# Hybrid SSD/GLA layer: the last block's final state updates left out, the last head's copies and scalings marked as high priority, and its two stores issued by GpSimd

## The chip, the cores and the metric

The kernel runs on 1 core of one Trainium2 chip. The metric is the device time of one execution in microseconds. Before the change it is 2318.2 us, the median of three runs (2316.95, 2318.2 and 2320.6).

A core has the engines TensorE (PE, matmuls; its weight loads are shown as PEld), VectorE (DVE), ScalarE (ACT), GpSimd (POOL) and SyncE (SP), which here only issues DMAs. ACT, too, issues DMAs, as instructions in its own stream (shown as ACTq). Each engine executes its instructions in order.

## The reference, cut to what matters

One layer (DEPTH = 1) over 16 meta tokens and 2048 real tokens, model width 1024. `u` is the normalised input, `proj = u @ w_in` feeds two branches; both carry a state from one chunk of tokens to the next, starting with the meta tokens:

```python
# SSD branch: 4 groups of 4 heads x 64 columns, chunk of 128 tokens
def step(s, inp):
    st, dec = inp
    return dec[..., None, None] * s + st, s          # state for the NEXT chunk
final, prev = lax.scan(step, state0, (states, chunk_decay))
y_off = einsum('bzthn,bzhpn,bhzt->bzthp', cc, prev, exp(da_cum))
return (y_diag + y_off), final
...
y_r, _ = ssd_chunked(...)                            # the last state is not used

# GLA branch: 4 heads, 128 key columns and 256 value columns each
def step(s, inp):
    qi, ki, vi, gi = inp
    o = (qi * exp(gi)) @ s + att(qi, ki, gi) @ vi
    s_new = exp(g_last)[..., None] * s + k_dec.T @ vi
    return s_new, o
...
o_r, _ = gla_chunked(...)                            # the last state is not used

y_gla = rmsnorm(o, gla_norm_w) * silu(g_gla)
merged = sum over branches of sigmoid(gate_b(u)) * (y_b @ w_branch[b])
out = rmsnorm(h + merged @ w_out, final_norm_w)      # float32 throughout
```

## The kernel before, in words

**Numbers.** A float32 product is made of three passes on PE: each operand is split into a high and a low part of type fp32r, and the helper `accum` (L189, L190, L191) sums hi*hi, lo*hi and hi*lo in PSUM. Small products (L594, L595, L597, L847) are plain float32 matmuls; the trace counts each as 2 instructions.

**Phase 1** (tile pools called `first`) goes over 4 blocks of 512 tokens (`nblk`), each of 4 chunks of 128 tokens (`NCH`). A block has 8 units: 4 SSD groups (`ssd_proj`, then `ssd_scan`) and 4 GLA heads (`gla_proj`, then `gla_scan`). They are generators: while one unit projects on PE, `step` lets the scans of earlier units go on one `yield` at a time. In `ssd_scan`, `after(c)` makes the output of chunk c (L594, L595) and the state behind it: a matmul (L597), a decay on POOL (L599) and an addition on DVE (L600). In `gla_scan` the last loop (L842 to L854) makes, for each chunk, in one PSUM bank `po`: the state product `kdt` x v in its right half (L845), the output in its left half (L846, L847), the state update on DVE (L848), a copy of the output to `ot` (ACT, L850) and the sum of its squares (ACT, L852). Then come the reciprocal root (`rstd_of`: DVE L232, POOL L233), four scalings of `ot` (ACT L857), eight transposes (PE L863, four for each half j), a product with the gate for each half (DVE L864, tile `gg`), and two stores of 256 KB into the scratch tensors `y_<block>_<number>` (L867, issued by ACT). For the last head of the last block these are y_3_6 and y_3_7; they are read again only for the last sums of the second branch, much later.

**Phase 2** (pools called `second`) has 7 stages (gate, branch 0 and branch 1 for each half of the tokens, then the output projection), each a row of block products by a scheme with 7 in place of 8 multiplications. A stage reads 28 right-hand tiles: `load_b` (L955, SP) into the raw ring `br` of 5 buffers, `prep_b` splits it by a copy on ACT (L960) and a subtraction on DVE (L961). The left-hand tiles: `load_a` (L967, SP) into the ring `ar` of 8 buffers, sums on POOL (L975 to L978), and `prep_a` splits them on ACT (L984) and DVE (L985). `product` is PE (`accum` again, bank `psa` or `psb`), with a snapshot on ACT (L1001) behind some. A gate stage adds on DVE (L1012), takes tanh on ACT (L1019) and stores with a DMA that ACT issues (L938).

**What sets the order.** PE and SP execute in the order of the code (`manual_schedule`). The instructions of ACT, DVE and POOL are put in order by a scheduler, which plays the program through with its own costs; `tc.high_priority()` puts what stands in it ahead of what else is ready there. Where phase 1 ends, ACT and DVE already hold phase 2's first `prep_a`, ahead of or between the last head's steps. A tile of phase 2 lies in memory that phase 1 had, and waits for whoever used it last.

**Counters of the DMAs.** The DMAs that SP and ACT issue take turns, in the scheduler's order over both engines, on eight completion counters, DMAHW0 to DMAHW7. A DMA whose counter is still out waits until the transfer that had it before, eight DMAs earlier, has landed. DMAs that POOL issues have counters of their own (DMASW).

## Time and profile before

| what | value |
|---|---|
| median of 3 runs | 2318.2 us (2316.95 to 2320.6) |
| the profiled execution's own time | 2309.24 us |
| its span (first to last instruction) | 2307.5 us |
| TensorE clock granted, mean | 0.993 |
| PE busy | 2229.4 us, 97% of the span |
| DVE, ACT, POOL busy | 1623.4, 1119.5, 682.3 us (70%, 49%, 30%) |
| DMA | 515.89 MB, mean 224 GB/s |

An answer of the trace is read as follows. A row of a timeline has the start in us from the span's start, the duration, the engine, the line, the operation, output<-input, size, xcount (instructions that were grouped), and in brackets how long the engine was idle ahead of it and who ended that. A row of a table by windows has the window, its length, then busy time and instructions of PE, PEld, DVE, ACT and POOL, the granted TensorE clock, the busy share of the DMA engines and GB/s. Phase 1 ends and phase 2 begins at about 1501 us; this place is called the seam below.

### The profile page before, as it was taken

The page shows a single profiled execution, that of the slowest core. Times are in us where ns is not written, and L with a number is a line of the kernel's source. Part 1 is how long each engine was busy: PE and PEld are TensorE (multiplying, and loading weights), DVE is VectorE, ACT ScalarE, POOL GpSimd, SP SyncE. Part 2 cuts the span into 40 slices and gives each one's busy share as a digit, 9 for nine tenths or more (in the row PEclk, how much of TensorE's full clock was granted, in tenths as well). Part 3 has the DMA queues.
Part 4 walks back from the last instruction along what each step waited for, and adds up shares of the span by engine and source line. Part 5 has one row for each costly group of instructions (what it writes and reads, how often), then busy time and mean ns, then how long its engine had stood idle before and what let it go on. Part 6 is the DMA issues. An engine that isn't in the chain of part 4 may idle for free.

```text
span 2307.5 us, 36497 instructions
## 1 busy us (share of the span) xinstructions
PE 2229.4 (97%) x12651; PEld 1947.3 (84%) x12651; DVE 1623.4 (70%) x3144; ACT 1119.5 (49%) x2508; POOL 682.3 (30%) x677
## 2 busy tenths in 40 slices
PE   6899999999999999999999999989999999999998
PEld 6899988888889889888988898868788788787886
DVE  5787866687775677676578666664679854788876
ACT  5565654454444454444455334464554455454443
POOL 3344433122221122211122100136424264423341
PEclk9999999999999999999999999999999999999999
DMA  7766865667786676886667655466768866778653
GB/s 255 230 220 214 305 228 204 201 203 233 261 279 197 204 229 204 266 279 208 205 216 228 206 166 162 143 212 214 236 230 270 290 222 215 251 260 271 226 192 110
DMA packets 300937, 515.89 MB, mean 224 GB/s; under 512 B 27616, under 2 KB 143584, under 8 KB 300752
## 3 DMA queue, kind: packets, MB, share of 16 engines
q1 hardware_dynamic: 221840, 422.15, 56.1%
q10 hardware_dynamic: 78912, 91.41, 11.4%
q8 instruction: 99, 1.62, 0.3%
q14 instruction: 86, 0.70, 0.1%
HBM read 366.26 MB, written 147.19 MB: 223 GB/s over the span
## 4 chain that ended last, share of the span: by engine, by line
PE 68%; DVE 11%; DMA 9%; issue 5%; ACT 3%; POOL 2%; SPq 1%; ACTq 0%; DVEq 0%; POOLq 0%
PE pj L189 11%; PE pj L191 11%; PE pj L190 11%; PE psa L189 5%; PE psa L190 5%; PE psa L191 5%; PE psb L189 2%; PE psb L190 2%; PE psb L191 2%; PE pc L594 2%; DMA acc<-in_xmt 2%; PE pc L757 1%; DVE acc L508 1%; PE psc L189 1%; PE psc L190 1%
## 5 line engine op out<-in xcount | busy, mean ns | idle before, releaser
L189 PE MATMUL pj<-u,whl 128*128 128x512 f32 (+1 forms) x1184 | 445.5, 376 | 9.4 <-ACT acc L504 4.9
L191 PE MATMUL pj<-u,whl 128*128 128x512 f32 (+1 forms) x1184 | 430.1, 363 | 0.8 <-POOL whl L177 0.8
L190 PE MATMUL pj<-u,whl 128*128 128x512 f32 (+1 forms) x1184 | 429.3, 363 | 0.0
L189 PE MATMUL pj<-whl,u 128*128 128x256 f32 (+1 forms) x992 | 288.7, 291 | 3.2 <-ACT u L252 2.2
L191 PE MATMUL pj<-whl,u 128*128 128x256 f32 (+1 forms) x992 | 282.4, 285 | 0.2 <-DVE u L257 0.2
L190 PE MATMUL pj<-whl,u 128*128 128x256 f32 (+1 forms) x992 | 282.1, 284 | 0.4 <-POOL whl L177 0.4
L189 PE MATMUL psa<-b,a 128*128 128x512 f32 x640 | 252.4, 394 | 19.3 <-ACT sn L1001 15.8
L189 PEld LDWEIGHTS pj<-u,whl 128*128 128x128 f32 x1184 | 224.1, 189 | 47.9 <-ACT acc L504 5.7
L191 PEld LDWEIGHTS pj<-u,whl 128*128 128x128 f32 x1184 | 223.6, 189 | 36.6 <-POOL whl L177 1.1
L190 PEld LDWEIGHTS pj<-u,whl 128*128 128x128 f32 x1184 | 224.3, 189 | 33.2
L190 PE MATMUL psa<-b,a 128*128 128x512 f32 x640 | 251.3, 393 | 0.0
L191 PE MATMUL psa<-b,a 128*128 128x512 f32 x640 | 251.0, 392 | 0.0
L985 DVE TENSOR_TENSOR a<-ar,a 128x512 fp32r<-128x512 f32 x160 | 158.8, 1000 | 74.2 <-ACT a L984 73.9
L80 POOL TENSOR_TENSOR wr<-wr 128x256 f32<-128x256 f32 x80 | 68.4, 855 | 440.1 <-DMA wr<-u 179.8
L189 PEld LDWEIGHTS pj<-whl,u 128*128 128x128 f32 x992 | 189.6, 191 | 4.3 <-ACT u L252 2.4
L177 POOL TENSOR_TENSOR whl<-wr,whl 128x512 fp32r<-128x512 f32 (+1 forms) x100 | 136.5, 1372 | 190.7 <-ACT whl L176 151.4
L190 PEld LDWEIGHTS pj<-whl,u 128*128 128x128 f32 x992 | 189.8, 191 | 1.0 <-POOL whl L177 0.6
L191 PEld LDWEIGHTS pj<-whl,u 128*128 128x128 f32 x992 | 189.6, 191 | 0.8 <-DVE u L257 0.8
L961 DVE TENSOR_TENSOR b<-br,b 128x512 fp32r<-128x512 f32 x196 | 148.9, 781 | 40.2 <-ACT b L960 39.6
L975 POOL TENSOR_TENSOR as<-ar,ar 128x512 f32<-128x512 f32 x40 | 58.0, 1450 | 399.5 <-DMA ar<-in_w_br 134.2
L508 DVE SCALAR_TENSOR_TENSOR acc<-cin,hcw,acc 128x512 f32<-128x512 f32 (+1 forms) x192 | 159.4, 830 | 13.9 <-ACT acc L504 11.8
L960 ACT ACTIVATE b<-br 128x512 fp32r<-128x512 f32 x196 | 118.9, 626 | 94.3 <-DMA br<-br_t 33.0
(280 smaller groups left out, 5026.6 us busy)
## 6 DMA issues: line engine op xcount, KB each, us to landing
whl<-k_s SPq DMA_DIRECT2D x96, 512.0 KB, 4.4
whl<-k_g SPq DMA_DIRECT2D x96, 512.0 KB, 4.1
whl<-k_v SPq DMA_DIRECT2D x48, 512.0 KB, 4.1
whl<-k_z SPq DMA_DIRECT2D x36, 512.0 KB, 4.2
wr<-in_w_feat SPq DMA_DIRECT2D x64, 256.0 KB, 4.3
k_s<-whl SPq DMA_DIRECT2D x32, 512.0 KB, 3.7
cb<-cumd ACTq DMA_DIRECT2D x64, 256.0 KB, 5.8
y<-gg ACTq DMA_DIRECT2D x64, 256.0 KB, 4.7
```

Of the source, the lines that this page charges most:

```text
L80: nc.gpsimd.tensor_tensor(o, x, y, op=ALU.subtract)
L177: nc.gpsimd.tensor_tensor(hl[:, 1], raw, hl[:, 0].bitcast(F32), op=ALU.subtract)
L189: nc.tensor.matmul(ps, sh, mh, start=first, stop=False, **kw)
L190: nc.tensor.matmul(ps, sh, ml, start=False, stop=False, **kw)
L191: nc.tensor.matmul(ps, sl, mh, start=False, stop=last, **kw)
L508: nc.vector.scalar_tensor_tensor(acc, cin[:, k:k + tt], hcw[:, ti, k:k + 1], acc, op0=ALU.mult, op1=ALU.add)
L594: nc.tensor.matmul(py[:, h * 64:(h + 1) * 64], dm[:, h], xdt[:, h], start=True, stop=True)
L757: nc.tensor.matmul(ps[:, r * P:(r + 1) * P], kq[:, 2 * r * P:(2 * r + 1) * P], kq[:, (2 * r + 1) * P:(2 * r + 2) * P], start=True, stop=True)
L960: nc.scalar.activation(t[:, 0], raw, AF.Copy)
L961: nc.vector.tensor_tensor(t[:, 1], raw, t[:, 0].bitcast(F32), op=ALU.subtract)
L975: nc.gpsimd.tensor_tensor(s1, a21, a22, op=ALU.add)
L985: nc.vector.tensor_tensor(t[:, 1], src, t[:, 0].bitcast(F32), op=ALU.subtract)
```

## The change

1. In `ssd_scan`, `after(c)` leaves out L597, L599 and L600 for the last chunk of the last block (in each of 4 groups).
2. In `gla_scan`, the loop leaves out the `kdt` product (L845, 3 PE instructions) and the state update (L848) for the last chunk of the last block (in each of 4 heads). Both states are read by nobody after that.
3. For the last head of the last block, the state updates, copies, sums of squares, reciprocal root and scalings (L848 to L857) stand in `tc.high_priority()`.
4. That head's two stores are issued by GpSimd in place of ScalarE.

```diff
@@ -593,11 +593,12 @@
             for h in range(4):
                 nc.tensor.matmul(py[:, h * 64:(h + 1) * 64], dm[:, h], xdt[:, h], start=True, stop=True)
             nc.tensor.matmul(py[:, 256:512], cf[:, a:a + P], s_ssd[:, g], start=True, stop=True)
-            pst = bank(pc, "pc")
-            nc.tensor.matmul(pst[:, :256], bt, xw.rearrange("p a c -> p (a c)"), start=True, stop=True)
-            sv = s_ssd[:, g].rearrange("p (h c) -> p h c", c=64)
-            nc.gpsimd.tensor_tensor(sv, sv, hb(dec[:, ci, hs], P), op=ALU.mult)
-            nc.vector.tensor_tensor(s_ssd[:, g], s_ssd[:, g], pst[:, :256], op=ALU.add)
+            if c < NCH - 1 or o.b < nblk - 1:
+                pst = bank(pc, "pc")
+                nc.tensor.matmul(pst[:, :256], bt, xw.rearrange("p a c -> p (a c)"), start=True, stop=True)
+                sv = s_ssd[:, g].rearrange("p (h c) -> p h c", c=64)
+                nc.gpsimd.tensor_tensor(sv, sv, hb(dec[:, ci, hs], P), op=ALU.mult)
+                nc.vector.tensor_tensor(s_ssd[:, g], s_ssd[:, g], pst[:, :256], op=ALU.add)
             yo = mk(wk, [P, 4, 64], F32, "c1", bufs=NC1)
             nc.vector.tensor_tensor(yo, py[:, 256:512].rearrange("p (h c) -> p h c", c=64),
                                     hb(ecu[:, ci, hs], P), op=ALU.mult)
@@ -839,22 +840,32 @@
 
         ot = mk(wk, [P, NCH, 256], F32, "ot", bufs=1)
         ssq = mk(sm, [P, 4], F32, "ssq")
+        very_last = o.b == nblk - 1 and h == GH - 1
+
+        def urgent():
+            return tc.high_priority() if very_last else nullcontext()
+
         for c in range(NCH):
+            more = c < NCH - 1 or o.b < nblk - 1
             po = bank(pc, "pc")
             vc = [t[:, c] for t in got["v"][0]]
-            accum(po[:, 256:], [t[:, c] for t in kdt], vc, True, True)
+            if more:
+                accum(po[:, 256:], [t[:, c] for t in kdt], vc, True, True)
             accum(po[:, :256], [t[:, c] for t in atp], vc, True, False)
             nc.tensor.matmul(po[:, :256], qg[:, c * P:(c + 1) * P], s_gla[:, h], start=False, stop=True)
-            nc.vector.scalar_tensor_tensor(s_gla[:, h], s_gla[:, h], egl[:, c:c + 1], po[:, 256:],
-                                           op0=ALU.mult, op1=ALU.add)
-            nc.scalar.activation(ot[:, c], po[:, :256], AF.Copy)
-            jk = mk(wk, [P, 256], BF16, "junk", bufs=1)
-            nc.scalar.activation(jk, po[:, :256], AF.Square, accum_out=ssq[:, c:c + 1])
+            with urgent():
+                if more:
+                    nc.vector.scalar_tensor_tensor(s_gla[:, h], s_gla[:, h], egl[:, c:c + 1], po[:, 256:],
+                                                   op0=ALU.mult, op1=ALU.add)
+                nc.scalar.activation(ot[:, c], po[:, :256], AF.Copy)
+                jk = mk(wk, [P, 256], BF16, "junk", bufs=1)
+                nc.scalar.activation(jk, po[:, :256], AF.Square, accum_out=ssq[:, c:c + 1])
             if c % 2:
                 yield
-        r = rstd_of(ssq, 4, 1.0 / 256)
-        for c in range(NCH):
-            nc.scalar.activation(ot[:, c], ot[:, c], AF.Identity, scale=r[:, c:c + 1])
+        with urgent():
+            r = rstd_of(ssq, 4, 1.0 / 256)
+            for c in range(NCH):
+                nc.scalar.activation(ot[:, c], ot[:, c], AF.Identity, scale=r[:, c:c + 1])
         yield
         gs = got["gs"]
         for j in range(2):
@@ -864,7 +875,7 @@
             nc.vector.scalar_tensor_tensor(gs[j], ps, hgw[:, j:j + 1], gs[j], op0=ALU.mult, op1=ALU.mult)
         yield
         for j in range(2):
-            nc.scalar.dma_start(y_left[1][o.b][2 * h + j], gs[j])
+            (nc.gpsimd if very_last else nc.scalar).dma_start(y_left[1][o.b][2 * h + j], gs[j])
 
 
     running, begun = [], []
```

Behind the first edit, the lines of the changed kernel have numbers higher by 1 to 11: L600 is L601 there, L850 and L852 are L860 and L862, L857 is L868, L867 is L878, L955 is L966, L960 is L971, L967 is L978, L984 is L995, L1001 is L1012.

**First place: ACT, the last head's copies.** `ot<-pc` is the copy of a chunk (two rows for chunks 0 and 1, then chunk 2, then chunk 3), `junk,ssq<-pc` its sum of squares, `a<-ar` and `a<-as` are phase 2's first splits, y_3_4 and y_3_5 the stores of the head before. Before:

```order
L867 DMA y_3_4_156<-gg_16909 128x512 [waits DMAHW6_49,DVE_49]
L867 DMA y_3_5_157<-gg_16987 128x512 [waits DMAHW0_49,DVE_49]
L850 ACTIVATE ot_17148<-pc_17186 128x256 [waits DVE_49]
L852 ACTIVATE junk_17196,ssq_17149<-pc_17186 128x256 [waits Activation_49]
L984 ACTIVATE a_17434<-ar_17388 128x512
L984 ACTIVATE a_17449<-ar_17375 128x512 [waits DMAHW5_49]
L984 ACTIVATE a_17460<-ar_17390 128x512 [waits DMAHW1_49]
L984 ACTIVATE a_17475<-as_17382 128x512 [waits Pool_49]
L850 ACTIVATE ot_17148<-pc_17198 128x256 [waits DVE_49]
L852 ACTIVATE junk_17208,ssq_17149<-pc_17198 128x256 [waits Activation_49]
```

After:

```order
L878 DMA y_3_4_156<-gg_16885 128x512 [waits DMAHW6_49,DVE_49]
L878 DMA y_3_5_157<-gg_16963 128x512 [waits DMAHW0_49,DVE_49]
L995 ACTIVATE a_17402<-ar_17356 128x512
L995 ACTIVATE a_17417<-ar_17343 128x512 [waits DMAHW5_49]
L995 ACTIVATE a_17428<-ar_17358 128x512 [waits DMAHW1_49]
L860 ACTIVATE ot_17120<-pc_17158 128x256 [waits DVE_49]
L862 ACTIVATE junk_17168,ssq_17121<-pc_17158 128x256 [waits Activation_49]
L995 ACTIVATE a_17443<-as_17350 128x512 [waits Pool_49]
L860 ACTIVATE ot_17120<-pc_17170 128x256 [waits PE_49]
L862 ACTIVATE junk_17176,ssq_17121<-pc_17170 128x256 [waits Activation_49]
```

Chunk 2's copy, which stood ahead of three splits of phase 2, now stands behind them; the copy of chunk 3 has kept its place behind four splits.

**Second place: ACT, from the last head's scalings to phase 2's first right-hand tile.** `ot<-ot,rstd` is a scaling (the last of four), `b<-br` the first splits of right-hand tiles. Before:

```order
L857 ACTIVATE ot_17148<-ot_17148,rstd_17212 128x256 [waits Activation_49]
L984 ACTIVATE a_17533<-as_17397 128x512 [waits Pool_49]
L984 ACTIVATE a_17551<-ar_17377 128x512
L867 DMA y_3_6_158<-gg_17075 128x512 [waits DMAHW3_49,DVE_49]
L867 DMA y_3_7_159<-gg_17138 128x512 [waits DMAHW4_49,DVE_49]
L960 ACTIVATE b_2979_17411<-br_17403 128x512 [waits DMAHW7_49]
L960 ACTIVATE b_2980_17414<-br_17405 128x512 [waits DMAHW7_49,DMAHW5_49]
```

After:

```order
L868 ACTIVATE ot_17120<-ot_17120,rstd_17180 128x256 [waits Activation_49]
L995 ACTIVATE a_17501<-as_17365 128x512 [waits Pool_49]
L995 ACTIVATE a_17519<-ar_17345 128x512
L971 ACTIVATE b_2975_17379<-br_17371 128x512 [waits DMAHW7_49,DMAHW4_49]
L971 ACTIVATE b_2976_17382<-br_17373 128x512 [waits DMAHW7_49,DMAHW5_49]
```

The two stores, which wait for DVE, are gone from between the splits. On POOL they now stand, as `L878 DMA`, behind L989 (which was L978) of phase 2's second left-hand pair and ahead of L986 (which was L975) of the third.

**Third place: SP, the loads of the third and fourth left-hand pair** (`ar<-in_w_feat`), right behind the last loads of the first stage's right-hand tiles (`br<-gate_t`); the counters in brackets are those that the load waits for. Before, DMAHW6 and DMAHW2 in the rows of ar_17682 and ar_17732 were held by the stores g_0_0 and g_0_2 (L938), the first two results of phase 2:

```order
L955 DMA br_17615<-gate_t_2_166 128x512 [waits DMAHW5_49,DVE_49]
L955 DMA br_17617<-gate_t_3_167 128x512 [waits DMAHW7_49,DVE_49]
L967 DMA ar_17682<-in_w_feat 128x512 [waits DMAHW6_49,Pool_49]
L967 DMA ar_17684<-in_w_feat 128x512 [waits Pool_49]
L967 DMA ar_17686<-in_w_feat 128x512 [waits DMAHW0_49,Pool_49]
L967 DMA ar_17720<-in_w_feat 128x512 [waits DMAHW1_49,Pool_49]
L967 DMA ar_17732<-in_w_feat 128x512 [waits DMAHW2_49]
```

After, DMAHW2 in the row of br_17583 is held by g_0_0 and DMAHW6 in that of ar_17654 by g_0_2:

```order
L966 DMA br_17583<-gate_t_2_166 128x512 [waits DMAHW4_49,DMAHW2_49,DVE_49]
L966 DMA br_17585<-gate_t_3_167 128x512 [waits DMAHW5_49,DVE_49]
L978 DMA ar_17650<-in_w_feat 128x512 [waits Pool_49]
L978 DMA ar_17652<-in_w_feat 128x512 [waits Pool_49]
L978 DMA ar_17654<-in_w_feat 128x512 [waits DMAHW6_49,Pool_49]
L978 DMA ar_17688<-in_w_feat 128x512 [waits DMAHW7_49,Pool_49]
L978 DMA ar_17700<-in_w_feat 128x512 [waits DMAHW0_49]
```

With two DMAs fewer on the eight counters, the waits for those two stores stand at other loads: for g_0_0 two loads earlier, and for g_0_2 at the third in place of the fifth left-hand load. From some 35 loads behind the first of these on, every load of SP waits for the same store in both programs.

2 lines of the change are left out of this document (1 added, 1 removed).

## The prediction

> **What bounds the kernel now.** I read the page first, then the waits and the timelines of the engines at the places that the diff touches, then the chain behind the seam. The page's first part says that TensorE is busy nearly all the time:
>
> ```profile
> PE 2229.4 (97%) x12651; PEld 1947.3 (84%) x12651; DVE 1623.4 (70%) x3144; ACT 1119.5 (49%) x2508; POOL 682.3 (30%) x677
> ```
>
> So work that is taken from another engine is worth nothing unless PE waits for it, and work taken from PE is worth its whole length, unless PE then waits for something else. The waits of PE from 1240 to 1500 us, where three of the four SSD scans of the last block end and all its GLA heads run (waited-for line, sum, times, longest):
>
> ```profile
> PE pc L757 <- ACT junk L852: 1.3, 3, 0.6
> PE pc L189 <- ACT junk L852: 0.9, 1, 0.9
> PE pc L847 <- DVE s_gla L848: 0.2, 1, 0.2
> ```
>
> That is 2.4 us in 260. There PE sets the pace, and no transfer is waited for. The one long hole is the seam. PE's timeline there:
>
> ```profile
> 1499.74 0.28 PE L190 MATMUL pc<-tok,kdt 128*128 128x256 f32 x1
> 1499.85 0.28 PE L191 MATMUL pc<-tok,kdt 128*128 128x256 f32 x1
> ...
> 1500.36 0.70 PE L847 MATMUL pc<-s_gla,act 128*128 128x256 f32 x2
> 1505.90 2.53 PE L863 MATMUL pt<-cst,ot 128*128 128x128 f32 x8 [4.84 <-ACT ot L857]
> 1511.91 0.80 PE L189 MATMUL psa<-b,a 128*128 128x512 f32 x1 [3.47 <-ACT b L960]
> ```
>
> PE has finished phase 1's products at 1501.06, waits 4.84 us for ACT's scalings, transposes, and waits 3.47 us for phase 2's first tile. In these holes ACT and DVE are the path. ACT's rows:
>
> ```profile
> 1498.98 0.98 ACTq L867 DMA_DIRECT2D y<-gg  x2
> 1500.34 0.38 ACT L850 ACTIVATE ot<-pc 128x256 f32<-128x256 f32 x1 [1.38 <-DVE s_gla L848]
> ...
> 1503.06 0.38 ACT L850 ACTIVATE ot<-pc 128x256 f32<-128x256 f32 x1
> ...
> 1507.48 0.62 ACT L984 ACTIVATE a<-ar 128x512 fp32r<-128x512 f32 x1
> 1508.40 2.78 ACTq L867 DMA_DIRECT2D y<-gg  x2
> 1511.22 2.71 ACT L960 ACTIVATE b<-br 128x512 fp32r<-128x512 f32 x5 [3.13 <-DVE gg L864]
> ```
>
> And DVE's:
>
> ```profile
> 1507.62 0.75 DVE L864 SCALAR_TENSOR_TENSOR gg<-pt,hgw,gg 128x512 f32<-128x512 f32 x1 [3.40 <-PE pt L863]
> 1508.29 1.27 DVE L985 TENSOR_TENSOR a<-as,a 128x512 fp32r<-128x512 f32 x1
> 1509.48 0.68 DVE L985 TENSOR_TENSOR a<-ar,a 128x512 fp32r<-128x512 f32 x1
> 1510.08 0.74 DVE L864 SCALAR_TENSOR_TENSOR gg<-pt,hgw,gg 128x512 f32<-128x512 f32 x1
> 1511.89 3.10 DVE L961 TENSOR_TENSOR b<-br,b 128x512 fp32r<-128x512 f32 x5 [1.07 <-ACT b L960]
> ```
>
> A window of the seam (length, five busy times, clock, DMA share, GB/s), in which no transfer is under way:
>
> ```profile
> 1504.00:1505.00 1.00, 0.00 (x0) 0.00 (x0) 0.22 (x2) 0.00 (x0) 0.70 (x1) 1.00 0.00 0
> ```
>
> So phase 2's first loads, as many as the rings hold, have landed by then. The two stores hold ACT from 1508.40 until DVE has made the second half of `gg` (1510.82), and only then may ACT split the first right-hand tile, for which DVE then waits 1.07 us.
>
> **The change part by part.**
>
> *SSD states (4 groups).* The last of them on PE:
>
> ```profile
> 1225.06 0.65 PE L595 MATMUL pc<-s_ssd,act 128*128 128x256 f32 x2
> 1225.55 0.59 PE L597 MATMUL pc<-c,bt 128*128 128x256 f32 x2
> 1225.79 0.47 PE L189 MATMUL pj<-whl,u 128*128 128x256 f32 x1
> ```
>
> L595 ends at 1225.71 and L597 at 1226.14, so the pair takes 0.43 us of the stream; four make 4 x 0.43 = 1.72 us. PE works without a hole there, so I take all of it. The next row bounds it from the other side: L189 is done at 1226.26, 0.12 us behind L597, as if nothing had to be refilled. The POOL and DVE operations that go (4 each) lay beside PE: nothing.
>
> *GLA states (4 heads).* The three matmuls start 0.11 to 0.12 us apart, 0.35 us a product. Heads 0 to 2 are in PE's full stretch: 3 x 0.35 = 1.05 us. The state update that goes with it also held up ACT, which reads the same bank after DVE. In head 1 that reached PE; the copy of its last chunk, and the wait that followed:
>
> ```profile
> 1461.29 0.38 ACT L850 ACTIVATE ot<-pc 128x256 f32<-128x256 f32 x1 [1.50 <-DVE s_gla L848]
> 1462.09 1.16 PE L757 MATMUL pc<-sq 128*128 128x128 f32 x8 [0.43 <-ACT junk L852]
> ```
>
> Without the update nothing holds that copy 1.50 us, and the 0.43 us go: 1.48 us in all. Ends: 1.05 (the next bank is late as well), and 1.05 + 2.2 = 3.25 if all of PE's waits for `junk` went, which the other four do not promise, since they stand behind other chunks. The fourth head's product counts nothing: its chunk 3 waits for chunk 2's state, not for PE.
>
> *High priority.* The order puts chunk 2's copy behind three splits of phase 2, and leaves chunk 3's behind four. By itself it moves nothing forward. What it does is fill a hole: ACT has issued y_3_5 at 1499.96 and then idles 0.38 us until chunk 2 is ready; with the splits there it is full from 1499.96 on, chunk 3's sum, the root, the scalings, the transposes and the second half of `gg` all come 0.38 us earlier (chunk 3's L848, which the change drops, would have been done by then). It is a gain of the order, not of the priority.
>
> *Stores to POOL.* With them gone, ACT runs from its last split (1507.48, so 1507.1, until 1507.7) into the first right-hand tiles, whose loads have landed. DVE's first L961 then waits for DVE alone: the second half of `gg` starts at 1510.08 - 0.38 = 1509.70, and L961 follows at about 1510.4 in place of 1511.89. So the first complete tile comes 1.5 us earlier, 0.38 of it included. On POOL the two issues cover nobody's work:
>
> ```profile
> 1507.75 1.26 POOL L978 TENSOR_TENSOR as<-ar,as 128x512 f32<-128x512 f32 x1
> 1543.14 1.29 POOL L975 TENSOR_TENSOR as<-ar,ar 128x512 f32<-128x512 f32 x1 [34.14 <-DMA ar<-in_w_feat]
> ```
>
> POOL has 34.14 us without work behind the place where they stand, so what they take on POOL costs 0, whatever they take up to that; without that hole it would be at least the 0.98 us that ACT needs to issue two. The trace has no DMA issued by POOL. The nearest row for its landing is the same store from ACT:
>
> ```profile
> y<-gg ACTq DMA_DIRECT2D x64, 256.0 KB, 4.7
> ```
>
> [...]
>
> *Does the 1.5 us survive?* Behind the seam the chain of waits goes through loads that wait for a free `br` buffer, so each link moves with the first L961. Later links of it (with the issue of one DMA, 0.33 us), then the row of SP's eight left-hand loads, ACT's row and PE's wait there:
>
> ```profile
> 1533.41 4.49 DMA g<-sn
> 1537.91 5.73 DMA ar<-in_w_feat
> ...
> 1544.85 0.33 ACTq L938
> ...
> 1535.58 6.76 SPq L967 DMA_DIRECT2D ar<-in_w_feat  x8
> ...
> 1543.66 0.64 ACT L984 ACTIVATE a<-ar 128x512 fp32r<-128x512 f32 x1 [1.48 <-DMA ar<-in_w_feat]
> ...
> 1545.87 0.50 PE L189 MATMUL psa<-b,a 128*128 128x512 f32 x1 [0.62 <-ACT sn L1001]
> ```
>
> Here the fifth left-hand load waited for the store g_0_2 to land, for no reason but its counter. In the changed order the third load waits for it, and ACT issues that store two right-hand tiles earlier (ahead of the twenty-first of 28, not the twenty-third). SP began with these loads at 1535.58, so at 0.33 us an issue the fifth can come at 1536.9, 1.0 us earlier, and PE's 0.62 us wait can go. Ends: 0.62 gained, or, if the store still lands last, two loads more stand behind it, about 2 x 0.33 = 0.66 lost. I take 0.4 gained. So the seam gives 1.5 + 0.4 = 1.9 us.
>
> Sum: 1.72 + 1.48 + 1.9 = **5.1 us**. The profiled execution took 2309.24 us; by this it would take 2304.1. The median of the runs before lies 9 us above it, so I carry the difference over: 2318.2 - 5.1 = **2313.1 us**. About 0.2%, 4.6 us, is what a measurement of this kernel can tell from no change, and the forecast lies just beyond that.
>
> *The clock.* The granted clock at the seam and at another hole (window, length, five busy times, clock, DMA):
>
> ```profile
> 1505.00:1506.00 1.00, 0.10 (x1) 0.10 (x1) 0.00 (x0) 0.66 (x2) 1.00 (x2) 0.90 0.00 0
> 1506.00:1516.00 10.00, 6.53 (x17) 4.36 (x18) 6.46 (x10) 5.43 (x11) 3.00 (x3) 0.50 0.38 125
> ...
> 1970.00:1973.20 3.20, 0.04 (x1) 0.00 (x0) 1.84 (x2) 1.76 (x4) 3.12 (x4) 1.00 0.91 325
> 1973.20:1977.00 3.80, 3.77 (x10) 2.98 (x11) 3.80 (x5) 2.61 (x6) 3.80 (x3) 0.55 0.61 210
> ```
>
> A mean of 0.90 in the first row means half clock from about 1505.8, so the transposes and the first ten matmuls of phase 2 run at half speed. The hole that PE keeps is 4.84 - 0.38 = 4.46 us; the other one, of 3.2 us up to 1973.2, cost the clock too. I therefore leave the clock as it is.
>
> **The rivals.**
>
> *1. The clock stays up through the shorter hole.* The transposes would take about half of their 2.53 us; the four of the first half start DVE's row at 1507.62, 1.7 us behind their start, so everything behind comes about 0.8 us earlier: 5.1 + 0.8 = 5.9 us, 2312.3 us. The ten slow matmuls behind would add little, since PE waits for the ring's loads later. For it: the clock fell only 0.1 us before the transposes. Against it: a hole of 3.2 us was enough elsewhere. [...] Chance 0.12.
>
> *2. The seam's gain is given back on DVE.* POOL's stores would be issued from 1510.4 on, beside DVE's five L961 (3.10 us). Beside POOL's L978 a subtraction of the same kind took 1.27 us (the row at 1508.29), against 0.68 us for the next one: 0.6 us more for each that overlaps. Two or three so stretched take 1.2 to 1.8 us, and the seam gives 0.1 to 0.7 us: 3.3 to 3.9 us in all, about 2314.6 us. Against it: part of the 1.27 may be a wait for its input from ACT or POOL. [...] If PE could not keep the SSD gain either (a transfer of weights that has been just in time would have to hold it, and none is among its waits), 3.3 - 1.7 = 1.6 us are left. Chance 0.20.
>
> *3. The stores land late and the result is slower.* In the new order ACT's 26th and 27th right-hand tiles lie in the memory of `gg` and wait for POOL's two stores. These splits are at about 1538 before. With the stores released at 1510.4, the wait decides from a landing after about 1537, 26 us later, where ACT's landed in 4.7. It makes the kernel slower than before when it exceeds the 5.1 gained, and measurably so at 9.7 us, a landing 36 us behind the issue: then 2322.8 us or more. For it speaks only that no such DMA is in the trace. Chance 0.06.
>
> *4. The change does less than it says.* For the priority that is so by the order, and it is in the sum; the rest cannot fail to happen, since the instructions are gone.
>
> **How the numbers follow.** Forecast 0.62, rival 1 0.12, rival 2 0.20, rival 3 0.06. The forecast's own range is 3.3 to 5.8 us (SSD 1.72; GLA 1.05 to 1.9, which is a second wait like head 1's; the counter -0.66 to 0.62; the rest of the seam 1.2 to 1.6, by 0.3 of unlike overlap), 2312.4 to 2314.9; I give 0.40 to its part beyond 4.6 us. Faster by over 0.2%: 0.40 + 0.12 = 0.52. Within 0.2%: 0.22 + 0.20 = 0.42. Slower: 0.06. The range runs from all of PE's waits for `junk` gone and the clock up (5.1 + 1.77 + 0.8 = 7.7 us, 2310.5) to rival 2's lower end (1.6 us, 2316.6), with 0.5 us more at either end for the medians, which come from runs up to 3.7 us apart: 2310.0 to 2317.1. Rival 3 is left out.
>
> **What would show it right or wrong.** In the profile after: no L597 in the last chunk's row, 12 fewer `kdt` matmuls; ACT without a gap between y_3_5 and the first split, and no wait for `gg` ahead of the first L971; the first L972 about 1.5 us closer to the end of phase 1's products (from 10.83 us behind 1501.06 to about 9.3 us); PE's wait near 1545.87 gone; POOL's hole still above 25 us. It is wrong if phase 1 does not end about 3 us earlier, if the L972 beside POOL's stores take over 1 us each, if a split of ACT waits for a store of POOL, or if the distance from the first L972 to the 100% stretch of PE behind 1546 grows.

## The result and the profile after

| | before | after |
|---|---|---|
| median, 22 runs each | 2317.05 us (2310.84 to 2324.73) | 2310.63 us (2304.15 to 2317.51) |
| profiled execution: time, span | 2309.24, 2307.5 us | 2308.46, 2306.7 us |

The ratio is 0.9974 [0.9965, 0.9982], or 6.0 us less (4.2 to 8.1); it is worked out from all the runs, while the medians alone lie 6.4 us apart. A second comparison of the same two kernels (run e11_after, below) gave 0.9993 [0.9976, 1.0010], 1.6 us less, which can't be told from no change. The two profiled executions lie only 0.8 us apart, though the landmarks in them moved by 5 us. So a single execution's span can't show this change, and the first thing to learn was which lengths in a trace repeat. Two do to about 0.2 us, and both lie where the change is:

- **GLA**: from the first to the last start of the last block's 16 output products (L847, now L855). Before: 1500.36 - 1401.35 = 99.01 us.
- **seam**: from that last product to DVE's first subtraction of a right-hand tile (L961, now L972). Before: 1511.89 - 1500.36 = 11.53 us.

In two profiles of the changed kernel GLA is 98.56 and 98.58, the seam 9.31 and 9.11. What lies outside does not repeat: over all fourteen profiles, whatever the edit, the last block's first SSD product stood 1200.1 to 1206.5 us behind the span's start, and from the seam to the end it took 795.6 to 800.9 us. Lengths of all kernels:

| kernel | GLA | seam | time against before |
|---|---|---|---|
| before | 99.01 | 11.53 | 1 |
| after | 98.56 | 9.31 | 0.9974 [0.9965, 0.9982] |
| e1_states | 98.29 | 11.55 | 0.9983 [0.9970, 0.9996] |
| e2_store | 99.06 | 10.39 | 1.0003 [0.9989, 1.0017] |
| e3_prio | 99.29 | 10.78 | 0.9992 [0.9979, 1.0005] |
| e4_noprio | 98.37 | 10.40 | 0.9986 [0.9972, 0.9999] |
| e5_filler | 98.90 | 9.23 | 0.9979 [0.9962, 0.9996] |
| e6_warm | 98.63 | 9.22 | 0.9979 [0.9961, 0.9997] |
| e7_sp | 98.67 | 10.00 | 0.9993 [0.9975, 1.0010] |
| e8_pool | 98.65 | 10.92 | 1.0000 [0.9983, 1.0016] |
| e9_bfirst | 98.67 | 7.49 | 0.9951 [0.9938, 0.9964] |
| e10_both | 98.59 | 6.91 | 0.9982 [0.9965, 0.9999] |
| e11_after | 98.58 | 9.11 | 0.9993 [0.9976, 1.0010] |
| e12_bfirst | 98.64 | 7.61 | 0.9990 [0.9974, 1.0007] |

The first part of the changed kernel's page: PE has lost 20 instructions (8 of the SSD products, 12 passes of the GLA products), and its busy time is not less (2229.4 before); the mean granted clock of this execution was 0.990, that of before was 0.993.

```profile
PE 2232.1 (97%) x12631; PEld 1949.0 (84%) x12631; DVE 1609.6 (70%) x3136; ACT 1121.4 (49%) x2508; POOL 683.6 (30%) x675
```

PE at the last SSD chunk, after. L597's row is gone: L189 now starts 0.30 us behind L595, where it started 0.73 us behind it (1225.06 to 1225.79), 0.43 us less. The other three groups show the same two numbers.

```profile
1224.52 0.65 PE L595 MATMUL pc<-s_ssd,act 128*128 128x256 f32 x2
1224.82 0.47 PE L189 MATMUL pj<-whl,u 128*128 128x256 f32 x1
```

PE's waits from 1238 to 1498 us, after (line waited for, sum, times, longest). They come to 3.4 us, where they were 2.4. The first line was one wait of 0.2; the second was 0.9.

```profile
PE pc L855 <- DVE s_gla L858: 1.2, 5, 0.3
PE pc L189 <- ACT junk L862: 1.2, 1, 1.2
PE pc L758 <- ACT junk L862: 0.6, 1, 0.6
PE pc L758 <- DVE c L765: 0.4, 1, 0.4
```

The seam, after, engine by engine. PE:

```profile
1497.36 0.70 PE L855 MATMUL pc<-s_gla,act 128*128 128x256 f32 x2 [0.23 <-DVE s_gla L858]
1501.83 2.53 PE L874 MATMUL pt<-cst,ot 128*128 128x128 f32 x8 [3.77 <-ACT ot L868]
1504.59 0.79 PE L189 MATMUL psa<-b,a 128*128 128x512 f32 x1 [0.23 <-ACT b L971]
1507.40 0.79 PE L190 MATMUL psa<-b,a 128*128 128x512 f32 x1 [2.02 <-DVE b L972]
```

ACT:

```profile
1495.84 0.59 ACTq L878 DMA_DIRECT2D y<-gg  x1
1496.48 1.67 ACT L995 ACTIVATE a<-ar 128x512 fp32r<-128x512 f32 x3 [0.64 <-DVE gg L875]
1498.05 0.36 ACT L860 ACTIVATE ot<-pc 128x256 f32<-128x256 f32 x1
...
1501.27 1.71 ACT L868 ACTIVATE ot<-ot,rstd 128x256 f32<-128x256 f32 x4 [1.33 <-POOL rstd L233]
...
1503.40 0.62 ACT L995 ACTIVATE a<-ar 128x512 fp32r<-128x512 f32 x1
1503.92 2.69 ACT L971 ACTIVATE b<-br 128x512 fp32r<-128x512 f32 x5
```

DVE:

```profile
1503.54 0.75 DVE L875 SCALAR_TENSOR_TENSOR gg<-pt,hgw,gg 128x512 f32<-128x512 f32 x1 [3.40 <-PE pt L874]
1504.21 1.28 DVE L996 TENSOR_TENSOR a<-as,a 128x512 fp32r<-128x512 f32 x1
1505.41 0.68 DVE L996 TENSOR_TENSOR a<-ar,a 128x512 fp32r<-128x512 f32 x1
1506.01 0.74 DVE L875 SCALAR_TENSOR_TENSOR gg<-pt,hgw,gg 128x512 f32<-128x512 f32 x1
1506.67 3.08 DVE L972 TENSOR_TENSOR b<-br,b 128x512 fp32r<-128x512 f32 x5
```

POOL, with the two stores:

```profile
1503.66 1.28 POOL L989 TENSOR_TENSOR as<-ar,as 128x512 f32<-128x512 f32 x1
1504.88 0.76 POOL L878 DMA_DIRECT2D y<-gg  x1
1507.06 0.55 POOL L878 DMA_DIRECT2D y<-gg  x1 [1.42 <-DVE gg L875]
1538.05 1.29 POOL L986 TENSOR_TENSOR as<-ar,ar 128x512 f32<-128x512 f32 x1 [30.44 <-DMA ar<-in_w_feat]
```

ACT goes from y_3_5 into the splits (0.05 us apart, though the row calls the time of the issue a wait for `gg`), has no hole before chunk 2's copy, and runs from the last left-hand split straight into the right-hand tiles. DVE's five subtractions follow the second half of `gg` by 0.66 us and wait for nothing. PE now starts its first product before DVE is through (its first pass needs only ACT's half of the tile) and then waits 2.02 us for L972. The third left-hand pair on POOL came 1538.05 - 1506.67 = 31.38 us behind the first L972, where it came 31.25 us behind it: what the seam gained had arrived there almost whole.

So the changed kernel lost 4 x 0.43 = 1.7 us in the SSD groups, 0.45 in GLA and 2.22 in the seam: 4.4 us, which lies within both intervals of the time. The landmarks of single profiles scatter about that: from the block's first L595 to the first L972 it took 311.4 us before, 306.3 after and 307.5 in e11_after, 5.2 and 3.9 us less. The difference lies among the first SSD chunks, ahead of what the change removes.

The SSD part has no experiment of its own, but a length bears it out: from the block's first L595 to the first output product of GLA it took 200.84 to 201.13 us in the three profiles that compute the states, and 198.39 to 200.21 us in the eleven that don't, 1.5 us less in the mean. Whether the 4.4 us reach the end of the kernel can't be seen in single traces, since what lies behind the seam scatters by 5 us. The times say that by and large they do: over all thirteen comparisons of the table the lengths (with 1.72 us for the SSD states) add up to 50.1 us less than before, and the ratios to 45.2.

### The profile page after: what moved, and what is told of

It is laid out like the page before. It is cut to its first block, busy times and chain, and to the rows that moved or that the text cites. A ratio compares the mean times of both kernels' runs of the same rounds, so it can differ in the third digit from the quotient of the medians.

```text
span 2306.7 us, 36436 instructions
## 1 busy us (share of the span) xinstructions
PE 2232.1 (97%) x12631; PEld 1949.0 (84%) x12631; DVE 1609.6 (70%) x3136; ACT 1121.4 (49%) x2508; POOL 683.6 (30%) x675
## 4 chain that ended last, share of the span: by engine, by line
PE 64%; DVE 12%; DMA 12%; issue 6%; ACT 4%; POOL 1%; SPq 1%; ACTq 0%; DVEq 0%; POOLq 0%
PE pj L189 11%; PE pj L191 11%; PE pj L190 11%; PE psa L189 4%; PE psa L190 4%; PE psa L191 4%; DMA acc<-in_xmt 2%; PE psb L190 2%; PE psb L189 2%; PE psb L191 2%; DMA br<-br_t 2%; PE pc L594 2%; PE pc L758 1%; DVE b L972 1%; PE psc L190 1%
## 5 line engine op out<-in xcount | busy, mean ns | idle before, releaser
L189 PE MATMUL pj<-u,whl 128*128 128x512 f32 (+1 forms) x1184 | 446.0, 377 | 9.5 <-ACT acc L504 4.5
L189 PE MATMUL pj<-whl,u 128*128 128x256 f32 (+1 forms) x992 | 288.7, 291 | 2.4 <-ACT u L252 2.2
L189 PE MATMUL psa<-b,a 128*128 128x512 f32 x640 | 254.0, 397 | 16.4 <-ACT sn L1012 16.2
L189 PEld LDWEIGHTS pj<-u,whl 128*128 128x128 f32 x1184 | 224.5, 190 | 48.4 <-ACT acc L504 5.4
L996 DVE TENSOR_TENSOR a<-ar,a 128x512 fp32r<-128x512 f32 x160 | 148.1, 930 | 84.3 <-ACT a L995 84.1
L189 PEld LDWEIGHTS pj<-whl,u 128*128 128x128 f32 x992 | 189.6, 191 | 4.1 <-ACT u L252 2.3
L972 DVE TENSOR_TENSOR b<-br,b 128x512 fp32r<-128x512 f32 x196 | 148.4, 780 | 43.2 <-ACT b L971 43.1
L986 POOL TENSOR_TENSOR as<-ar,ar 128x512 f32<-128x512 f32 x40 | 59.4, 1484 | 396.2 <-DMA ar<-in_w_br 154.2
L971 ACT ACTIVATE b<-br 128x512 fp32r<-128x512 f32 x196 | 119.3, 626 | 93.4 <-DMA br<-br_t 41.4
```

What stands on the lines that cost most here:

```text
L189: nc.tensor.matmul(ps, sh, mh, start=first, stop=False, **kw)
L971: nc.scalar.activation(t[:, 0], raw, AF.Copy)
L972: nc.vector.tensor_tensor(t[:, 1], raw, t[:, 0].bitcast(F32), op=ALU.subtract)
L986: nc.gpsimd.tensor_tensor(s1, a21, a22, op=ALU.add)
L996: nc.vector.tensor_tensor(t[:, 1], src, t[:, 0].bitcast(F32), op=ALU.subtract)
```

## Experiments

Kernels e1 to e4 take the change apart. e1 and e4 to e12 leave out the same unread states, e2 and e3 compute them. e5 and e6 add products that nobody reads, and e9, e10 and e12 add a zero to two tiles; no other computation differs.

**e1_states**: the changed kernel with only its skipped states.

```diff
-            return tc.high_priority() if very_last else nullcontext()
+            return nullcontext()
-            (nc.gpsimd if very_last else nc.scalar).dma_start(...)
+            nc.scalar.dma_start(...)
```

> Only the states are left out: the high priority and the stores' move to GpSimd are undone. My theory (the three parts add up, each read where it ends): the last product of phase 1 (before: L847 at 1500.36 us, after: L855 at 1497.36) starts at about 1497.1, since the copies of chunks 0 and 1 stand in the old order again, and the first split of phase 2 on DVE (before 1511.89, after 1506.67) at about 1508.4, 3.5 us ahead of before; the time is 3 to 4 us shorter than before. Rival (phase 1 is not what shortened the kernel; the median's 6.4 us come from the loads' new counters in phase 2): the landmarks move the same, but the time by 3.5 us less than the changed kernel's, or not at all.

GLA fell by 0.72 us, the seam not at all (11.55). With the four SSD products (1.72) the states are worth 2.4 us, and the time agrees (0.9983, 0.9 to 6.9 us).

**e2_store**: before, with only the two stores on GpSimd.

```diff
-            nc.scalar.dma_start(...)
+            (nc.gpsimd if o.b == nblk - 1 and h == GH - 1 else nc.scalar).dma_start(...)
```

> Only the last head's two stores are moved to GpSimd; all states are computed, and no priority is set. My theory: the last product stays at 1500.4, the first split of phase 2 on DVE follows the second half of gg at once, at about 1510.7 in place of 1511.89 (1.15 us earlier), and the time is 1 to 1.5 us shorter than before, which a measurement hardly tells from nothing. Rival (the new counters of the loads are worth as much again): 2.5 us or more shorter, with the first split at the same 1510.7.

The seam fell by 1.14 us, to 10.39; GLA stayed. The time can't be told from before (1.0003): 1.14 us lies inside the interval.

**e3_prio**: the changed kernel with its states computed and its stores on ScalarE.

```diff
-            if c < NCH - 1 or o.b < nblk - 1:
+            if True:
-            more = c < NCH - 1 or o.b < nblk - 1
+            more = True
-            (nc.gpsimd if very_last else nc.scalar).dma_start(...)
+            nc.scalar.dma_start(...)
```

> Only the high priority is set; all states are computed, and ACT issues the stores. My theory: the last product comes about 0.3 us later (chunk 2's bank waits for a sum of squares that now stands behind two copies), chunk 3's sum of squares ends about 0.4 to 0.6 us earlier since the splits fill ACT's hole, and the first split of phase 2 on DVE comes about 0.3 us earlier; the time is the same as before within 0.5 us. Rival (the priority is what made the seam shorter by 1 us more than forecast): first split 1 us or more earlier.

The seam fell by 0.75 us, and GLA grew by 0.28: 0.47 net.

**e4_noprio**: the changed kernel without the priority.

```diff
-            return tc.high_priority() if very_last else nullcontext()
+            return nullcontext()
```

> The changed kernel without the high priority. My theory: last product at about 1497.1, first split of phase 2 on DVE at about 1507.2 (the store's 1.15 us gained, the fill of ACT's hole not), 0.5 us later than in the changed kernel; the time is 4.5 us shorter than before, within 1 us of the changed kernel. Rival (the priority matters): the first split at 1508 or later, and the time 1.5 us or more above the changed kernel's.

The seam is 10.40, so the priority makes 1.09 us of it, against 0.19 that it costs in GLA: 0.90 net, over twice the 0.38 that was forecast. ACT of e4 shows why:

```profile
1503.08 0.33 ACTq L878 DMA_DIRECT2D y<-gg  x1
1504.33 0.38 ACT L860 ACTIVATE ot<-pc 128x256 f32<-128x256 f32 x1 [1.38 <-DVE s_gla L858]
...
1504.96 1.67 ACT L995 ACTIVATE a<-ar 128x512 fp32r<-128x512 f32 x3
```

y_3_5 is out at 1503.41, and ACT idles until 1504.33 with three splits behind it that wait for nothing: 0.92 us. The forecast took the hole from before, where that issue ended 0.38 us ahead of the copy. The hole is 0.37 us in e2, where only the stores are moved, and 0.83 in e1, where only the states are left out, so it is the states that widened it. DVE's split ahead of `gg` took 1.24 us before, beside a sum on POOL (L975, 1496.47 to 1497.74). In the changed kernel it took 0.68 us: it started at 1493.78, and POOL's last sum there had ended at 1493.58. In e1 it took 0.68 us too, and `gg` and y_3_5 are earlier. That split before, and in e1:

```profile
1497.05 1.24 DVE L985 TENSOR_TENSOR a<-ar,a 128x512 fp32r<-128x512 f32 x1
1499.07 0.68 DVE L996 TENSOR_TENSOR a<-ar,a 128x512 fp32r<-128x512 f32 x1
```

In the changed kernel phase 2's splits fill the hole. With the states computed the priority gave 0.47 net (e3), close to the forecast; with them left out it gave twice that. What it costs stands in PE's row of the changed kernel; before, this wait was 0.89:

```profile
1495.38 0.38 PE L189 MATMUL pc<-tok,kdt 128*128 128x256 f32 x1 [1.16 <-ACT junk L862]
```

With priority the copies of chunks 0 and 1 stand as a pair ahead of both sums of squares, and the sum that PE waits for is 0.27 us later:

```profile
1494.30 0.66 ACT L860 ACTIVATE ot<-pc 128x256 f32<-128x256 f32 x2 [2.31 <-PE pt L874]
1494.85 0.39 ACT L862 ACTIVATE junk<-pc 128x256 bf16<-128x256 f32 x1
```

**e5_filler**: the last chunk's product `kdt` x v is made again in each head, without the state update.

```diff
-            if more:
+            if True:
                 accum(po[:, 256:], [t[:, c] for t in kdt], vc, True, True)
```

> The changed kernel, but the last chunk's key-value product of the four heads is computed again (12 matmuls whose result nobody reads); the state update on DVE stays out. My theory (those matmuls had lain in a wait of PE for the state of the chunk before, which the changed kernel shows as 0.22 to 0.31 us ahead of each last chunk): from the first to the last state product of the heads it takes 98.56 us in the changed kernel, and here 0.3 to 0.6 us more, about 99.0. Rival (each product costs its whole 0.35 us, as in my prediction): 1.4 us more, 100.0. From the last product to phase 2's first split on DVE as in the changed kernel, 9.3 us.

Four products cost 0.34 us in GLA, not four times 0.35. The spacing of the output products tells where: from head 1's last product to the next it is 17.89 us before, 17.50 here and 17.19 after, and no other spacing differs between this kernel and the changed one by more than 0.02. The update had cost 0.39 there, the product 0.31. From chunk 2's to chunk 3's output product, where the removed one stood, it takes what it took in every head (1.17, 1.17, 1.27 and 1.17 us before, within 0.01 of that after). After, PE waits there for chunk 2's state, 0.22 to 0.31 us in each head. Head 1's rows:

```profile
1456.26 0.70 PE L855 MATMUL pc<-s_gla,act 128*128 128x256 f32 x2 [0.22 <-DVE s_gla L858]
1457.04 0.71 PE L758 MATMUL pc<-sq 128*128 128x128 f32 x4
```

Before, at the same place, no wait ahead of L847, and one behind it:

```profile
1458.86 0.70 PE L847 MATMUL pc<-s_gla,act 128*128 128x256 f32 x2
1459.84 0.71 PE L757 MATMUL pc<-sq 128*128 128x128 f32 x4 [0.29 <-ACT junk L852]
```

**e6_warm**: 13 products of 128x512 behind phase 1's last, which nobody reads, to keep the clock up.

```diff
+        if very_last:
+            warm = bank(pj, "pj")
+            for _ in range(13):
+                nc.tensor.matmul(warm, kdt[0][:, 3], kdt[0].rearrange("p c t -> p (c t)"), start=True, stop=True)
         with urgent():
             r = rstd_of(ssq, 4, 1.0 / 256)
```

> The changed kernel with 13 matmuls of 128x512 behind phase 1's last product, into a PSUM bank that nobody reads, about 3 us of work for PE in its hole of 3.77 us. My theory (the half clock costs time only where transposes lie on the path): the clock stays at 1.0 there, the eight transposes take 1.3 to 1.6 us in place of 2.53, phase 2's first split on DVE comes 0.5 to 0.9 us closer to the last product (9.3 before, 8.4 to 8.8 here), the first ten matmuls of phase 2 run in 0.23 us each; behind 1545 nothing more is gained. Rival (the clock is worth all its 3 to 4 us of slow matmuls): the time is 2.5 us or more below the changed kernel's.

The clock at the seam, first of the changed kernel (window, length, five busy times, clock, DMA share, GB/s):

```profile
1501.00:1502.00 1.00, 0.17 (x1) 0.17 (x1) 0.00 (x0) 0.73 (x2) 1.00 (x2) 0.78 0.00 0
1502.00:1511.00 9.00, 6.75 (x18) 4.40 (x19) 6.22 (x9) 5.15 (x11) 4.19 (x5) 0.50 0.39 136
```

and of e6, whose transposes start at 1505.45:

```profile
1505.00:1508.00 3.00, 1.75 (x8) 0.94 (x8) 0.98 (x2) 3.00 (x7) 3.00 (x3) 1.00 0.00 0
1508.00:1509.00 1.00, 0.49 (x1) 0.19 (x1) 1.00 (x1) 1.00 (x3) 1.00 (x2) 0.85 0.00 0
1509.00:1515.00 6.00, 3.98 (x9) 3.13 (x10) 4.56 (x9) 2.09 (x5) 0.81 (x2) 0.50 0.67 228
```

The clock stayed up through the transposes, and the seam is 9.22 us, no shorter than the 9.11 of e11 (8.4 to 8.8 was expected). The first half of `gg` came only 0.23 us earlier, since its four transposes follow ACT's four scalings (1.71 us) one by one. The second half came 0.69 us earlier, but from the first half of `gg` on, DVE has no idle time, and its four operations ahead of the first L972 (0.75, 1.42, 0.74 and 0.68 us) set it. The clock cost next to nothing there.

**e7_sp**: the two stores issued by SyncE.

```diff
-            (nc.gpsimd if very_last else nc.scalar).dma_start(...)
+            (nc.sync if very_last else nc.scalar).dma_start(...)
```

> The changed kernel with the last head's two stores issued by SyncE in place of GpSimd; there they stand right ahead of the sixth right-hand load, which waits for the first split anyway. My theory (only that ACT no longer issues them counts): from the last product to the first split on DVE 9.3 us as in the changed kernel, within 0.2, and the same time within 1 us. Rival (GpSimd's own queue and counters bring part of the gain): 0.5 us or more longer to the first split or to the 100% stretch of PE, and a time 1.5 us or more above the changed kernel's.

The seam is 10.00 us. Behind the second half of `gg` it is as in the changed kernel (13.06 to 13.72: 0.66 us); the 0.69 more came ahead of it. ACT's issue of y_3_5, a store that the edit does not touch, took 1.29 us for 0.59:

```profile
1502.20 1.29 ACTq L878 DMA_DIRECT2D y<-gg  x1
1503.53 1.67 ACT L995 ACTIVATE a<-ar 128x512 fp32r<-128x512 f32 x3 [1.34 <-issue]
```

Why it did stays open, with one profile. Without the extra 0.70 us the seam would be about 9.3, as in the changed kernel and as expected. The same issue took 0.39 us in e11, and there the seam is 0.20 us shorter than in the first profile: by these three profiles the time of this one issue goes straight into the seam. The time (0.9993) can't be told from before.

The next kernels ask what the seam's path is now. In the changed kernel chunk 3's sum stands behind four splits of ACT, and the first right-hand tile behind the last two left-hand splits.

**e8_pool**: the copies of three left-hand tiles made by GpSimd.

```diff
-            nc.scalar.activation(t[:, 0], src, AF.Copy)
+            if self.name == "gate0" and (n, p) in ((1, 1), (0, 2), (1, 2)):
+                nc.gpsimd.tensor_copy(t[:, 0], src)
+            else:
+                nc.scalar.activation(t[:, 0], src, AF.Copy)
```

> A step further: the copies of three of phase 2's first left-hand tiles, which stand ahead of the last head's chunks 2 and 3 on ACT, are made by GpSimd. My theory (ACT is full from its stores to chunk 3's sum of squares, and that run sets the root's start): chunk 3's sum ends about 1.0 us earlier than in the changed kernel; on GpSimd two more operations stand ahead of the second pair's sums, so that ACT's next splits come 1 us later, and phase 2's first split on DVE comes 0.5 to 1.0 us closer to the last product (8.3 to 8.8 against 9.3); time up to 1 us below the changed kernel's. Rival (GpSimd's copies, and DVE made slow beside them, become the path): the first split at 9.3 us or later.

Chunk 3's sum came 1.09 us earlier, but POOL's own sums came later behind the copies, and ACT waited for them:

```profile
1505.87 0.63 ACT L998 ACTIVATE a<-as 128x512 fp32r<-128x512 f32 x1 [2.33 <-POOL as L987]
```

The seam grew to 10.92 us. The path had gone to POOL.

**e9_bfirst**: the last two left-hand splits, (1,6) and (0,7), are tied to a zero made from the fourth right-hand tile, so that the order puts them behind the first right-hand tiles on ACT and DVE.

```diff
+    LATE = ((1, 6), (0, 7))
...
-            nc.scalar.activation(t[:, 0], src, AF.Copy)
+            if self.name == "gate0" and (n, p) in LATE:
+                zero = mk(spl, [P, 1], F32, "zero")
+                nc.vector.tensor_scalar(zero, self.b[1, 3][:, 1, 0:1].bitcast(F32), 0.0, 0.0, op0=ALU.mult, op1=ALU.add)
+                nc.scalar.activation(t[:, 0], src, AF.Identity, bias=zero)
+            else:
+                nc.scalar.activation(t[:, 0], src, AF.Copy)
```

> A step further, on the changed kernel: two of phase 2's left-hand splits (n1 p6 and n0 p7), which stand on ACT and DVE ahead of the first right-hand tile and are needed only six products later, are tied to a zero made from the fourth right-hand tile, so that they follow it. My theory (behind the first half of gg DVE is full until the first right-hand split, with 1.9 us of left-hand splits in between that nobody waits for): the first split on DVE comes 7.5 to 8.0 us behind the last product in place of 9.3, PE's wait of 2.0 us for it shrinks to under 1, and the time is 1 to 2 us below the changed kernel's. Rival (PE waits at the sixth product instead, or the loads' ring sets the pace from elsewhere): first split as early, but POOL's third pair and PE's 100% stretch no earlier than in the changed kernel.

DVE of e9 goes from both halves of `gg` into the right-hand tiles; L996's two rows, 1.28 and 0.68 us, are gone from between them:

```profile
1505.65 1.60 DVE L875 SCALAR_TENSOR_TENSOR gg<-pt,hgw,gg 128x512 f32<-128x512 f32 x2 [3.40 <-PE pt L874]
1507.17 3.09 DVE L974 TENSOR_TENSOR b<-br,b 128x512 fp32r<-128x512 f32 x5
```

The seam is 7.49 us, 1.82 less, and PE's wait for the first of these subtractions 1.02 in place of 2.02. The time is the best of all, 2305.55 us, 0.9951 [0.9938, 0.9964], from 6 runs.

**e10_both**: e9 and e8 together.

```diff
             if self.name == "gate0" and (n, p) in LATE:
...
+            elif self.name == "gate0" and (n, p) in ((1, 1), (0, 2), (1, 2)):
+                nc.gpsimd.tensor_copy(t[:, 0], src)
```

> The step before, and the three copies on GpSimd of the experiment e8_pool, which failed since ACT then waited for the second pair's sums; these now stand behind the right-hand tiles. My theory: chunk 3's sum of squares ends 1.0 us earlier than in the changed kernel, the first split on DVE comes about 6.7 to 7.1 us behind the last product, and the time is 2 to 3 us below the changed kernel's. Rival (GpSimd's copies make DVE slow or PE wait for a left-hand tile): first split at 7.5 us or later, or a new wait of PE for a left-hand tile that takes the gain.

The seam is the shortest, 6.91 us, but the five subtractions behind it took 5.78 us in place of 3.09, and PE waited for them twice (1.18 and 0.40 us):

```profile
1504.51 5.78 DVE L974 TENSOR_TENSOR b<-br,b 128x512 fp32r<-128x512 f32 x5
```

Beside them POOL was at its sums:

```profile
1503.54 1.28 POOL L989 TENSOR_TENSOR as<-as,ar 128x512 f32<-128x512 f32 x1
1504.77 1.73 POOL L990 TENSOR_TENSOR ar<-ar,ar 128x512 f32<-128x512 f32 x1
```

At 0.9982 it can't be told from the changed kernel: the landmark moved, and the tiles behind it gave it back. So the seam's length shows a gain only where the five subtractions behind it keep their time.

**e11_after** and **e12_bfirst**: the changed kernel and e9, unedited, once more and on one chip, since e9's gain was larger than its 1.8 us.

> The changed kernel once more, unedited, beside the next one on the same chip. My theory (its parts measured apart: SSD 1.7, GLA 0.7, stores 1.1, order by the priority 0.9, 4.4 us together): a ratio to before of 0.9981, within 0.9968 to 0.9994; from the last product to the first split on DVE 9.3 us. Rival (the 6 us of the first comparison are real, 1.6 of them in phase 2): 0.9974 or less.

> The kernel of e9_bfirst once more. My theory (its gain over the changed kernel is the 1.8 us by which the first split comes earlier): 1 to 3 us below the changed kernel beside it, a ratio to before of about 0.9973. Rival (0.9951 was real, so phase 2 gains 3 us more from loads that start earlier): 4 us or more below the changed kernel.

e11 is 0.9993 [0.9976, 1.0010] (medians 2313.39 and 2313.99 us), e12 0.9990 [0.9974, 1.0007] (2312.01). e12 is 1.4 us below e11 by the medians and 0.7 by the ratios, where their seams (9.11 and 7.61) differ by 1.5; the intervals overlap widely. So e9's median was below before's both times, and below the changed kernel's on the chip where both ran; by the seam it is 1.5 to 1.8 us better than the changed one, a size that no comparison of times here can show. What also stays open is why the change showed 6.0 us the first time and 1.6 the second; the parts, measured by lengths that repeat, come to 4.4.

## Why the prediction was right, and where its sum was not

The forecast was 5.1 us less, 2313.1 us; the median was 2310.63. The parts give 4.4, the two comparisons 6.0 and 1.6. The last product of phase 1 came 3.00 us earlier in the profile (1500.36 to 1497.36), as forecast, but the parts make only 1.72 + 0.45 = 2.2 of it, and the rest is scatter of the stretch ahead of them: that agreement was luck; the first L972 followed its end by 8.6 us (forecast 9.3).

**SSD, 1.72 us.** Right: 0.43 us for each group, and the length over all four groups fell by 1.5 in the mean.

**GLA, 1.48 us.** Half of it came, 0.72. The 0.43 us of head 1's wait behind the update came (0.39). The step that failed is "Heads 0 to 2 are in PE's full stretch: 3 x 0.35": it was read from a list of waits in which the product hid the wait. PE had the product to do while DVE made chunk 2's state; without it PE waits for that state, and the line of 0.2 us became 1.2. Only in head 1 did the product's removal come through, by 0.31. e5 shows it from the other side. The prediction said just this of the fourth head; it holds in the others too.

**Stores off ACT, 1.12 us.** Right: 1.14 (e2) and 1.15 (e1 to e4). What followed was DVE, as said.

**The order, 0.38 us.** The mechanism was right, the size not: 1.09 us in the seam, less 0.19 in GLA. "By itself it moves nothing forward" failed on a detail: it moved both first copies ahead of both sums, and PE paid for that. The hole's length was taken from the program before, and the first part of the change, the states, made the hole longer (0.38 to 0.92 us): the two parts are worth more together than apart.

**Counters, 0.4 us.** Did not come. From the chain after, and SP's row of the eight left-hand loads (6.76 us before):

```profile
1532.44 6.09 DMA ar<-in_w_feat
1529.89 4.65 SPq L978 DMA_DIRECT2D ar<-in_w_feat  x8
```

The fifth left-hand load was issued 0.25 us earlier against the first L972 (25.77 us behind it, before 26.02; 1.0 was forecast), its transfer then took 6.09 us for 5.73, and PE's product stands 34.10 us behind the first L972, before 33.98. The wait for the store did go (g_0_2 landed 22.70 us behind the first L972, ahead of all eight loads), but it had been worth less than forecast: the sum spaced SP's loads by 0.33 us, the length of ACT's issue, while they start 0.43 to 0.53 us apart, here the first two even 1.12. Before, the fifth load started 0.90 us behind the fourth, so the store had held it some 0.4 us. Nor is the 0.25 us sure: in e11 the same load came 26.45 us behind the first L972, later than before. PE's wait there is not gone, it grew from 0.62:

```profile
1540.77 0.50 PE L189 MATMUL psa<-b,a 128*128 128x512 f32 x1 [1.32 <-ACT sn L1012]
```

The forecast's 5.1 us and the 4.4 measured are near each other since what GLA and the counter lacked (0.8 and 0.4) and what the priority gave above 0.38 (0.90 - 0.38 = 0.5) partly cancel. That the sum came this close is in part luck.

**The rivals.** The clock (1) fell as before, half of full speed from about 1501.6 on, behind a hole of 3.77 us; and e6 shows that its 0.8 us would not have come either, since ACT's scalings paced the first transposes and DVE was full behind them. The seam's gain given back on DVE (2) did not happen: the five L972 took 3.08 us, before 3.10, though one of POOL's two issues (1507.06 to 1507.61) lay beside them; in e9 they took 3.09. It does happen beside POOL's sums, as e10 shows (5.78 us). The late stores (3): landing took 2.8 us, the changed kernel's row of DMA issues says, and no split of ACT waits for one.

```profile
y<-gg POOLq DMA_DIRECT2D x2, 256.0 KB, 2.8
```

## What to carry to other kernels

A product taken from a full PE is worth its length only if the operand of the next one is ready without it (here four products of 0.35 us gave 0.34 us together): look at who makes that operand and when, since a list of waits shows no wait that work still covers (0.2 us before, 1.2 after). When engines hand over between two phases, ask which one is full from the first partial result on; from there on, in the changed kernel, an earlier first result (by the priority, 1.09 us) or less work for that engine (e9, 1.82 us) moved the hand-over; feeding it faster behind the first result (the second half of `gg` in e6, 0.69 us earlier) moved nothing (9.22 us against 9.11 in e11). For a gain of 0.2%, measure lengths between landmarks that repeat, and add them up, rather than trust one execution's span.

## What the runs showed of the hardware

- **DVE beside POOL.** In the changed kernel's DVE rows a subtraction of 128x512 took 0.68 us at 1505.41, where POOL ran no sum. The one ahead of it took 1.28: it started at 1504.21 while POOL's L989 ran until 1504.94, and ended 0.55 us behind that. The `gg` operation, which reads one input from PSUM, took 0.75 at 1503.54, beside POOL's sums, and 0.74 at 1506.01, without. Beside one of POOL's DMA issues five subtractions took 3.08 us, before, with none, 3.10; in e10, beside three of POOL's sums (from 1503.54 to 1508.53) and its two issues, they took 5.78.
- **The clock in short holes.** In the changed kernel a hole of 2.65 us further on cost PE its clock:

```profile
1652.77:1655.40 2.63, 0.01 (x1) 0.00 (x0) 1.64 (x3) 1.77 (x4) 2.63 (x2) 0.96 0.83 266
1655.40:1658.40 3.00, 2.98 (x7) 2.42 (x8) 3.00 (x4) 2.25 (x5) 2.92 (x3) 0.50 0.80 298
```

  and before, at the same place, a longer one (2.94 us) did not:

```profile
1657.70:1660.60 2.90, 0.00 (x1) 0.00 (x0) 1.57 (x2) 1.76 (x4) 2.82 (x3) 1.00 0.87 292
1660.60:1664.00 3.40, 3.04 (x12) 2.17 (x12) 3.40 (x4) 2.21 (x5) 3.40 (x3) 1.00 0.70 231
```

  So the hole's length alone does not decide.

  In these two traces every change of the granted clock falls on one grid of 3.41 us, and between two changes inside the span it stays at half for 3.41, 6.83 or 10.24 us. The first hole fell almost whole into one stretch of that grid (1651.75 to 1655.17), in which PE was busy for 1.03 us; the clock is 0.50 in the next one and 1.00 again from 1658.58 on. Before, the hole lay across two (1655.98 to 1659.39 and 1659.39 to 1662.80), in which PE was busy for 1.72 and 2.16 us. In this the two holes differ; whether it is what decides, and from which busy share on the clock stays up, was not measured.
- **Stores from POOL.** An issue of 256 KB took POOL 0.76 and 0.55 us (ACT's last two in the same trace 0.33 and 0.59), and landed in 2.8 us, with no other transfer under way when the first was issued.
